# First norm's statistics from a second copy of the input, sums issued first, two convolutions held back, and the first output chunks by token halves

## The chip, the cores and the metric

The kernel runs on one core of a Trainium2 chip. Times are device microseconds of one launch. The kernel before took 2095.43 us as the median of three runs (2094.10 to 2096.46); a share of one thousandth is 2.1 us. The profiled execution is a run of its own.

The engines are named as the profile names them: PE is the matrix engine (PEld its weight loads), DVE the vector engine, ACT the scalar engine, POOL the general one, SP the one that issues the weight loads. Each works through its own list of instructions in order, and waits on the others by semaphores.

## The reference, cut to what matters

A decoder trunk of two layers on 256 tokens with 2048 features, in float32. Only the first mixer is touched by the change:

```python
u = rmsnorm(h, mix_pre_g[0])                       # h = x, 256 tokens by 2048
proj = u @ w_in                                    # 2048 by 3*2048
xin, gate_c, gate_b = jnp.split(proj, 3, axis=-1)
v = gate_c * xin
conv = sum(conv_w[k] * vp[:, k:k + S] for k in range(3))   # vp: v shifted right by 2, causal
m = (gate_b * conv) @ w_out
h = h + rmsnorm(m, mix_post_g[0])

def rmsnorm(x, g):
    return x * rsqrt(mean(x * x, axis=-1) + 1e-6) * g
```

Behind it come a squared-ReLU MLP (2048 to 8192 and back), the shared keys and values, stick-breaking attention and a second MLP. None of these is changed.

The factor `1/rms` of a token is the same for all features, so it commutes with the product by `w_in`. The kernel multiplies `x*g` by `w_in`, and scales afterwards: `gate_b` by r, and `gate_c*xin` by r squared, where r is the token's `1/rms`.

## The kernel before, in words

**Numbers in two parts.** Every float32 factor is split into a rounded high part and a remainder. ACT makes the high part of a weight chunk (`whi`, line 176), DVE the remainder (`wlo`, line 187). A chunk is 128 by 1024 numbers, 512 KB, loaded by SP into one of 5 `raw` buffers; 7 pairs of `whi`/`wlo` buffers hold split chunks and the splitting runs up to 4 chunks ahead of the product. So each chunk costs ACT and DVE one instruction over 128x1024 each.

**The input projection** (`convolution`) computes `w_in` with features on the partitions and the 256 tokens on the columns. Its units, in order:

- The **lead**: six column tiles of 128 features together, while the input arrives (k from 0 to 15, 12 chunks). Each lives in a bank of its own, banks 0 to 5.
- **Tiles 0 to 3**: one column tile each, two chunks each, in banks 0, 1, 7, 6.
- **Pair 0, tile 4, pair 1, tile 5, ... pair 15, tile 19.** A pair is two chunks of a second set of columns, computed with tokens on the partitions by a seven-product scheme. A pair needs four combinations of its weights (`sums`, line 213, DVE), their splits (`whi20a`, `b`, `t`, `u` for the pair whose first chunk is number 20), and four combinations of the input (`xs`, `xsums`). Eight pairs make a group, in banks 0 to 5 and 7; after pairs 7 and 15 DVE adds the group up (`mg<-mg,more` and `mg<-mg,acc`, line 988).
- **Tiles 20 to 25**, in banks 0, 1, 2, 0, 1, 3, with 16 transposes between tiles 21 and 22.

Tiles 3 to 19 share bank 6. A product with `whi` fills 512 columns (the input's high part and its remainder side by side), one with `wlo` 256, so a tile ends with `combined`: ACT copies the second half out (`half`, line 875), DVE adds it to the first (`sum`, line 877). The bank is free when that sum is done; the next tile in bank 6 starts one pair later. In tiles 0 and 2 and in tiles 20, 22 and 24 the `wlo` products stand ahead of the `whi` products.

**The convolutions.** Three sums (xin, gate_c, gate_b of one 128-feature block) go into `conv_tile`: a product (line 914), the scaling by r squared (921) and by r (926), the three taps (923 on ACT, 924, 925), the gate (927), and a split into the operand `y` (260 on ACT, 261). The eight blocks 0 to 7 come from the lead and tiles 0 to 17. The other eight come from tiles 18 to 25 (gates) and the pairs, after the transposes.

**Statistics.** While the lead runs, ACT squares the transposed input two feature blocks at a time (`sq`, line 891), DVE adds eight such tiles (`acc`, lines 893 and 895); then one addition (904), one product on PE with a matrix of 1/2048 (`ms`, 906), which sums over partitions and spreads the result, a root on ACT (908), a reciprocal (909) and a square (910) on DVE.

**The order.** On PE the order is the one in which the code is written. On DVE, ACT, POOL and SP a scheduler orders the instructions ahead of time, by the order of the code and by when its own model finds their inputs ready; `tc.high_priority()` lets an instruction pass others that are ready, `tc.issue_after(x)` puts it behind x.

**The output projection** (`project`, class `Mixed`) follows at once: chunks 96 to 127 of the stream, two groups of 16. For each chunk `both` calls `unit` for token half 0 (banks 0 and 1 in the first group) and then half 1 (banks 2 and 3); one half of a chunk is six products of 128x512.

Of the kernel before, what the change touches and what calls it, by code (L numbers as in the profile page):

```python
# [46 lines left out]
LATER = 7  # L47
# [3 lines left out]
DOWN_BANKS = {(0, 0): 3, (0, 1): 4, (1, 0): 5, (1, 1): UP_BANK, 1: 6, 5: 7, 6: 0, 7: 1}  # L51
LAST_BANKS = [[6, 7], [0, 1]]
OUT_MIXED = (((0, 1, 2, 5, 3, 6, 4, 7), (4, 6)), (tuple(range(KD // 2)), (3, 4)))
SEVEN = [((0, 1, 2, 3),) * 2] * (STEPS - 1) + [((0,), ())]
LOAD_FROM = 1
# [43 lines left out]
def trunk(ctx, tc, x, xT, vecs, rows, ws, out):  # L99
# [8 lines left out]
    wsplit = ctx.enter_context(tc.tile_pool(name="ws", bufs=RING))  # L108
    psum = ctx.enter_context(tc.tile_pool(name="ps", bufs=1, space=bass.MemoryType.PSUM))
# [250 lines left out]
    class Mixed(Group):  # L360


        def __init__(self, first, xs, banks, more, order, sevens_at, shared, evict):
            super().__init__(first, KD, xs, banks, self.add_and_evict)
            self.then, self.early = evict, 2 * sevens_at[-1] + 3 < KD - EDGE
# [12 lines left out]
        def both(self, i):  # L378
# [447 lines left out]
    def convolution(tmp):  # L826
# [27 lines left out]
        acc = tmp.tile([P, 2 * T], F32, tag="acc", name="acc", bufs=1)  # L854
# [17 lines left out]

        def combined(ps):
            b = tiny("half")
            nc.scalar.activation(b[:], ps[:, T:], AF.Copy)
            s = tiny("sum", bufs=LEAD + 2)
            nc.vector.tensor_tensor(s[:], ps[:, :T], b[:], op=ALU.add)  # L877
            return s
# [9 lines left out]
        def squares(q, behind):  # L888
            sq = tmp.tile([P, 2 * T], F32, tag="sq", name="sq", bufs=1)
            with tc.issue_after(entered[behind].ins):  # L890
                nc.scalar.activation(sq[:], hpair[q], AF.Square)
            if q == 0:
                nc.vector.tensor_copy(acc[:], sq[:])
            else:
                nc.vector.tensor_tensor(acc[:], acc[:], sq[:], op=ALU.add)

# [3 lines left out]
        mean = tmp.tile([P, P], F32, name="mean")  # L900
        nc.vector.memset(mean[:], 1.0 / D)

        def statistics():
            nc.vector.tensor_tensor(acc[:, :T], acc[:, :T], acc[:, T:], op=ALU.add)
            ps = bank(LEAD - 1, "ms")
            nc.tensor.matmul(ps[:, :T], mean[:], acc[:, :T], start=True, stop=True)
            r, r2 = tiny("rstd", bufs=1), tiny("rstd2", bufs=1)
# [25 lines left out]
        for k in range(KD):  # L933
# [12 lines left out]
            if k % 2 and LATER <= k + 2 < KD:  # L946
                squares((k + 2 - LATER) // 2, k + 2)
# [59 lines left out]
        for kind, i in IN_UNITS:  # L1007
# [23 lines left out]
            if i == KD + 3:  # L1031
                gated()
# [582 lines left out]
```

## Time and profile before

| what | value |
|---|---|
| runs, median (lowest to highest) | 2095.43 us (2094.10 to 2096.46) |
| profiled execution, its own time | 2094.54 us |
| its span, first to last instruction | 2092.7 us |
| granted PE clock | 0.999 |
| PE busy | 2079.6 us (99%) |
| DVE busy | 1896.7 us (91%) |
| ACT busy | 1466.4 us (70%) |
| end of the input projection, first product of the output projection | 269.48 us |

The busy times are shares of the whole span. The change touches the first 290 us or so, and there the question is which engine ends a wait last: an engine busy all the time can be the one that sets the pace, and PE can be the one that waits. In the answers of the trace, a row gives the start in us, the length, the engine, the line of the code, the instruction with output and inputs, and in brackets the idle time before it with the engine and line that ended it. Rows of one engine can overlap by about 0.08 us, since they are pipelined; the distance between two starts is what an instruction costs.

### The profile page before, as it was taken

The numbers are of one execution on the slowest core, as the hardware profiler recorded it, in microseconds if no ns is written. First come the engines' busy times: TensorE is split into PE (matmuls) and PEld (weight loads), VectorE is DVE, ScalarE is ACT, GpSimd is POOL, SyncE is SP. The second block draws the span as 40 slices with busy tenths as digits, with TensorE's granted clock in tenths as the row PEclk, the third lists the DMA queues.
The fourth block names the chain that finished last, engine by engine and source line by source line (L and its number), as shares of the span: only waits on it lengthen the run. The fifth ranks groups of instructions, "written<-read, shape, count | busy, mean of one in ns | idle before, by whom it ended". The sixth has DMA issues, their size and how long they took to land.

```text
span 2092.7 us, 29773 instructions
## 1 busy us (share of the span) xinstructions
PE 2079.6 (99%) x10564; PEld 1773.3 (85%) x10564; DVE 1896.7 (91%) x2822; ACT 1466.4 (70%) x2150; POOL 114.7 (5%) x141
## 2 busy tenths in 40 slices
PE   9999999999999999999999999999999999999998
PEld 7888888888888888888888888889888888888887
DVE  8999998999999999999766777558999999999996
ACT  8666556777777777777567888547877777777774
POOL 0000000000100101101000000000001010010010
PEclk9999999999999999999999999999999999999999
DMA  8466675677878878779575555665687787787884
GB/s 293 150 205 210 200 268 178 194 232 227 241 218 237 236 216 252 227 230 259 180 223 163 161 161 162 220 181 171 187 254 228 221 247 222 230 245 218 232 241 165
DMA packets 132917, 449.23 MB, mean 215 GB/s; under 512 B 14880, under 2 KB 15136, under 8 KB 132256
## 3 DMA queue, kind: packets, MB, share of 16 engines
q1 hardware_dynamic: 113328, 406.68, 60.8%
q0 software_dynamic: 19296, 40.38, 9.7%
q8 instruction: 83, 1.36, 0.3%
q14 instruction: 66, 0.54, 0.1%
q10 hardware_dynamic: 144, 0.26, 0.0%
HBM read 413.19 MB, written 2.10 MB: 198 GB/s over the span
## 4 chain that ended last, share of the span: by engine, by line
PE 96%; DVE 3%; issue 1%; DMA 0%; ACT 0%; SPq 0%; DVEq 0%; ACTq 0%
PE up L1138 21%; PE up L1145 12%; PE acc L334 7%; PE acc L336 7%; PE acc L335 7%; PE acc L868 5%; PE more L1252 5%; PE more L1251 5%; PE more L1253 5%; PE acc L1251 4%; PE acc L1252 4%; PE acc L1253 4%; PE lead L868 1%; PE up L1140 1%; PE tr L266 1%; DVE wlo L187 1%
## 5 line engine op out<-in xcount | busy, mean ns | idle before, releaser
L187 DVE TENSOR_TENSOR wlo<-raw,whi 128x1024 fp32r<-128x1024 f32 (+1 forms) x410 | 489.2, 1201 | 54.0 <-ACT whi L176 53.3
L176 ACT ACTIVATE whi<-raw 128x1024 fp32r<-128x1024 f32 (+1 forms) x410 | 421.4, 1044 | 139.9 <-PE acc L336 46.6
L1138 PE MATMUL up<-u,whi 128*128 128x512 f32 x1952 | 465.0, 389 | 0.0
L1138 PEld LDWEIGHTS up<-u,whi 128*128 128x128 f32 x1952 | 365.0, 188 | 74.7
L1145 PEld LDWEIGHTS up<-u,wlo 128*128 128x128 f32 x2048 | 263.6, 191 | 10.3
L1145 PE MATMUL up<-u,wlo 128*128 128x256 f32 x2048 | 268.0, 283 | 0.0
L213 DVE TENSOR_TENSOR sums<-raw,sums 128x512 f32<-128x512 f32 x260 | 177.3, 682 | 0.9
L189 DVE SCALAR_TENSOR_TENSOR wlo<-raw,gv,whi 128x512 fp32r<-128x512 f32 (+1 forms) x160 | 131.8, 853 | 41.5 <-ACT whi L176 40.8
L176 ACT ACTIVATE whi<-raw,gv 128x512 fp32r<-128x512 f32 (+1 forms) x160 | 121.6, 800 | 48.4 <-PE acc L336 42.0
L334 PE MATMUL acc<-whi,u 128*128 128x512 f32 x384 | 153.1, 399 | 0.1
L336 PE MATMUL acc<-whi,u 128*128 128x512 f32 x384 | 149.9, 390 | 0.0
L335 PE MATMUL acc<-wlo,u 128*128 128x512 f32 x384 | 149.7, 390 | 0.0
L1151 ACT ACTIVATE half<-up 128x256 f32<-128x256 f32 x128 | 49.1, 385 | 132.9 <-PE up L1145 130.4
L1158 POOL DMA_DIRECT2D mg<-more x108 | 94.0, 870 | 824.4 <-ACT more L1213 422.4
L868 PE MATMUL acc<-u,whi 128*128 128x512 f32 x416 | 98.9, 391 | 2.8 <-DVE sum L877 2.8
L868 PEld LDWEIGHTS acc<-u,whi 128*128 128x128 f32 x416 | 77.4, 188 | 20.5 <-DVE sum L877 3.7
L213 DVE TENSOR_TENSOR sums<-raw,raw 128x512 f32<-128x512 f32 x130 | 88.7, 682 | 3.8 <-DMA raw<-w_mlp 3.5
L213 DVE TENSOR_TENSOR sums<-raw 128x512 f32<-128x512 f32 x130 | 88.6, 681 | 1.3 <-DMA raw<-w_mlp 1.1
L336 PEld LDWEIGHTS acc<-whi,u 128*128 128x128 f32 x384 | 72.1, 188 | 15.5
L334 PEld LDWEIGHTS acc<-whi,u 128*128 128x128 f32 x384 | 72.2, 188 | 13.9 <-ACT tk L1446 0.6
L335 PEld LDWEIGHTS acc<-wlo,u 128*128 128x128 f32 x384 | 72.3, 188 | 13.3
L868 PEld LDWEIGHTS acc<-u,wlo 128*128 128x128 f32 x416 | 52.8, 191 | 3.8 <-DVE sum L877 2.1
(6789 smaller groups left out, 4607.0 us busy)
## 6 DMA issues: line engine op xcount, KB each, us to landing
raw<-w_mlp SPq DMA_DIRECT2D x512, 512.0 KB, 4.7
raw<-w_in SPq DMA_DIRECT2D x94, 512.0 KB, 4.4
mg<-more POOLq DMA_DIRECT2D x108, 256.0 KB, 6.1
raw<-w_out SPq DMA_DIRECT2D x32, 512.0 KB, 4.6
raw<-w_v SPq DMA_DIRECT2D x32, 512.0 KB, 4.3
raw<-w_k SPq DMA_DIRECT2D x32, 512.0 KB, 4.2
raw<-w_q SPq DMA_DIRECT2D x32, 512.0 KB, 3.8
raw<-w_wo SPq DMA_DIRECT2D x32, 512.0 KB, 3.7
```

The lines of the kernel that those rows point to most:

```text
L176: rounded = nc.scalar.activation(hi[:, at], raw[i][:, at], AF.Copy, scale=1.0 if gain is None else gain)
L187: nc.vector.tensor_tensor(lo[:, at], t[:, at], hi[:, at].bitcast(F32), op=ALU.subtract)
L213: nc.vector.tensor_tensor(t, x, y, op=ALU.subtract)
L334: nc.tensor.matmul(ps[:], xh, hi[:, a], start=first, stop=False, skip_group_check=skip)
L335: nc.tensor.matmul(ps[:], xh, lo[:, a], start=False, stop=False, skip_group_check=skip)
L336: self.done = nc.tensor.matmul(ps[:], xl, hi[:, a], start=False, stop=last, skip_group_check=skip)
L868: nc.tensor.matmul(ps[:, :cols], w, xs[:, :cols], start=k == 0 and part == parts[0], stop=k == KD - 1 and part == parts[1], skip_group_che ...
L1138: nc.tensor.matmul(ps, weight(0, first, m), x, start=k == 0, stop=False)
L1145: nc.tensor.matmul(pss[n][:, :T], weight(1, first, m), x, start=False, stop=k == KD - 1)
L1251: nc.tensor.matmul(self.ps[key][:], xh, hi, start=first, stop=False)
L1252: nc.tensor.matmul(self.ps[key][:], xh, lo, start=False, stop=False)
L1253: self.done = nc.tensor.matmul(self.ps[key][:], xl, hi, start=False, stop=last)
```

## The change

- **Statistics.** The squares of the transposed input, their additions, the product on PE, and the reciprocal over 128x256 are gone. The input is loaded a second time, as rows (tokens on the partitions), in four pieces of 512 KB from POOL's queue, each held behind the `half` of tile 0, 1, 1 and 2. ACT squares a piece in place and adds up along it (two pieces behind the `half` of tile 2, two behind that of tile 3). Two columns of sums are added, rooted and inverted per 128 tokens (128x1 each), turned by 32x32 transposes, written as a line of 256 numbers to a scratch tensor in DRAM, and read back to all partitions. Behind the `half` of tile 5 ACT makes r and r squared of it.
- **Sums.** In `combined`, both instructions get high priority.
- **Convolutions.** Three sums are put in a list; from tile 5 on, a convolution is taken from it per tile while more than two wait, from tile 20 on while any waits. Before, blocks 0, 2, 1, 3, 4, 5, 6, 7 were done at tiles 1, 2, 4, 5, 8, 11, 14, 17. Now blocks 0 to 7 are done at tiles 5, 6, 8, 11, 14, 17, 20, 21. The ring of sums has 12 buffers in place of 8.
- **Output projection.** In its first group, the first two chunks are done for token half 0 and then for half 1, in place of chunk by chunk.

```diff
-LATER = 7
+ROWS_AT = {0: (0,), 1: (1, 2), 2: (3,)}
+SQUARES_AT = {2: (0, 1), 3: (2, 3)}
+STATISTICS_AT = 3
+HELD = 2
+TURN = 32
...
+            self.first_by_half = not shared["sums"] and banks[0][0] == 0
...
-            if p not in self.at:
+            if p not in self.at and (i > 1 or not self.first_by_half):
                 super().both(i)
+            elif i == 0:
+                self.unit(0, 0)
+            elif i == 1:
+                self.unit(0, 1)
+                for n in range(2):
+                    self.unit(1, n)
...
         def combined(ps):
             b = tiny("half")
-            nc.scalar.activation(b[:], ps[:, T:], AF.Copy)
-            s = tiny("sum", bufs=LEAD + 2)
-            nc.vector.tensor_tensor(s[:], ps[:, :T], b[:], op=ALU.add)
+            with tc.high_priority():
+                copied["last"] = nc.scalar.activation(b[:], ps[:, T:], AF.Copy)
+            s = tiny("sum", bufs=LEAD + 6)
+            with tc.high_priority():
+                nc.vector.tensor_tensor(s[:], ps[:, :T], b[:], op=ALU.add)
             return s
...
+        def load_piece(q, behind):
+            b, c = q // 2, q % 2
+            if c == 0:
+                xrows.append(act.tile([P, D], F32, tag="x4", name="xrows"))
+            load = nc.gpsimd.dma_start(
+                xrows[b][:, c * D // 2 : (c + 1) * D // 2], x[b * P : (b + 1) * P, c * D // 2 : (c + 1) * D // 2]
+            )
...
+        def square_piece(q, behind):
...
+            a = xrows[b][:, c * D // 2 : (c + 1) * D // 2]
+            with tc.issue_after(behind.ins):
+                nc.scalar.activation(a, a, AF.Square, accum_out=sq[b][:, c : c + 1])
+
         def statistics():
-            nc.vector.tensor_tensor(acc[:, :T], acc[:, :T], acc[:, T:], op=ALU.add)
-            ps = bank(LEAD - 1, "ms")
-            nc.tensor.matmul(ps[:, :T], mean[:], acc[:, :T], start=True, stop=True)
-            r, r2 = tiny("rstd", bufs=1), tiny("rstd2", bufs=1)
-            nc.scalar.activation(r[:], ps[:, :T], AF.Sqrt, bias=eps[:])
-            nc.vector.reciprocal(r[:], r[:])
-            nc.vector.tensor_tensor(r2[:], r[:], r[:], op=ALU.mult)
-            scale["r"], scale["r2"] = r, r2
+            line = scratch.tile([1, T], F32, name="line")
+            turn = tmp.tile([P, NB * TURN], F32, name="turn")
+            with tc.high_priority():
+                for b in range(NB):
+                    nc.vector.tensor_tensor(sq[b][:, 0:1], sq[b][:, 0:1], sq[b][:, 1:2], op=ALU.add)
+                    r = inverse_root(sq[b][:, 0:1], eps[:])
+                    nc.vector.tensor_copy(roots[:, b * TURN : b * TURN + 1], r[:])
+                nc.vector.transpose(turn[:], roots[:])
+            nc.gpsimd.dma_start(
+                line[:].rearrange("o (b a t) -> (o a) b t", b=NB, t=TURN), turn[0:P:TURN, :].rearrange("a (b t) -> a b t", b=NB)
+            )
+            scale["all"] = tiny("rstd", bufs=1)
+            nc.gpsimd.dma_start(scale["all"][:], line[:].to_broadcast([P, T]))
+
+        def scales(behind):
+            r = scale["all"]
+            scale["r"], scale["r2"] = tiny("rstd1", bufs=1), tiny("rstd2", bufs=1)
+            with tc.issue_after(behind.ins):
+                nc.scalar.activation(scale["r"][:], r[:], AF.Copy)
+                nc.scalar.activation(scale["r2"][:], r[:], AF.Square)
...
-            if not scale:
+            s = combined(ps)
+            for q in ROWS_AT.get(i, ()):
+                load_piece(q, copied["last"])
+            for q in SQUARES_AT.get(i, ()):
+                square_piece(q, copied["last"])
+            if i == STATISTICS_AT:
                 statistics()
-            s = combined(ps)
+            if i == STATISTICS_AT + 2:
+                scales(copied["last"])
...
-                if lead and len(new) == 2:
-                    conv_tile(LEAD // 3 - len(lead) // 3, *lead[:3])
-                    del lead[:3]
                 if len(new) == 3:
-                    conv_tile(n - 2 * KD, *new)
+                    waiting.append((n - 2 * KD, *new))
                     new = []
+            if i >= STATISTICS_AT + 2 and len(waiting) > (0 if i >= KD + 4 else HELD):
+                conv_tile(*waiting.pop(0))
```

What this does to the lists, at two places. **DVE at the end of the lead** (`lead` names the lead's banks, the number behind `wlo` is the chunk). Before:

```order
L895 TENSOR_TENSOR acc_113<-acc_113,sq_479 128x512
L187 TENSOR_TENSOR wlo15_541<-raw15_407,whi15_540 128x1024
L895 TENSOR_TENSOR acc_113<-acc_113,sq_482 128x512
L187 TENSOR_TENSOR wlo16_547<-raw16_431,whi16_546 128x1024
L904 TENSOR_TENSOR acc_113<-acc_113 128x256
L187 TENSOR_TENSOR wlo17_561<-raw17_454,whi17_560 128x1024
L877 TENSOR_TENSOR sum_487<-lead_125,half_485 128x256
L877 TENSOR_TENSOR sum_491<-lead_126,half_489 128x256
```

Now:

```order
L279 TENSOR_TENSOR xs_648<-xa_645 128x128
L279 TENSOR_TENSOR xs_648<-xs_648,xa_645 128x128
L192 TENSOR_TENSOR wlo15_518<-raw15_396,whi15_517 128x1024
L279 TENSOR_TENSOR xs_648<-xa_645,xs_648 128x128
L192 TENSOR_TENSOR wlo16_524<-raw16_420,whi16_523 128x1024
L892 TENSOR_TENSOR sum_464<-lead_126,half_462 128x256
L892 TENSOR_TENSOR sum_468<-lead_127,half_466 128x256
L892 TENSOR_TENSOR sum_472<-lead_128,half_470 128x256
L953 TENSOR_TENSOR sum_464<-sum_464,sum_468 128x256
L192 TENSOR_TENSOR wlo17_538<-raw17_440,whi17_537 128x1024
```

The additions of squares are gone, the split of chunk 17 stands behind the first three sums, and two more sets of input combinations (`xs`, `xsums`) stand ahead of them than before.

**DVE from the sum of tile 20 on** (chunks 90 and 91 are tile 23, 92 and 93 tile 24; the first `sum` row of each piece is that of tile 20). Before:

```order
L877 TENSOR_TENSOR sum_2516<-acc_2469,half_2514 128x256
L187 TENSOR_TENSOR wlo90_2520<-raw90_2421,whi90_2519 128x1024
L187 TENSOR_TENSOR wlo91_2534<-raw91_2435,whi91_2533 128x1024
L919 MEMSET v_2589 128x2
L926 TENSOR_TENSOR sum_2369<-sum_2369,rstd_593 128x256
L919 MEMSET v_2602 128x2
L926 TENSOR_TENSOR sum_2463<-sum_2463,rstd_593 128x256
L926 TENSOR_TENSOR sum_2516<-sum_2516,rstd_593 128x256
L187 TENSOR_TENSOR wlo92_2640<-raw92_2474,whi92_2639 128x1024
L187 TENSOR_TENSOR wlo93_2654<-raw93_2488,whi93_2653 128x1024
L877 TENSOR_TENSOR sum_2565<-acc_2518,half_2563 128x256
```

Now, the first rows and, some 40 rows further on, those around chunks 92 and 93:

```order
L892 TENSOR_TENSOR sum_2493<-acc_2446,half_2491 128x256
L953 TENSOR_TENSOR sum_1751<-sum_1751,sum_1846 128x256
L958 MEMSET v_2496 128x2
L965 TENSOR_TENSOR sum_1941<-sum_1941,rstd1_1016 128x256
L960 TENSOR_TENSOR v_2496<-sum_1751,rstd2_1017 128x256
L192 TENSOR_TENSOR wlo90_2509<-raw90_2398,whi90_2508 128x1024
L963 SCALAR_TENSOR_TENSOR conv_2499<-v_2496,gv_83,conv_2499 128x256
L192 TENSOR_TENSOR wlo91_2523<-raw91_2412,whi91_2522 128x1024
```

```order
L266 TENSOR_TENSOR y4_2600<-sum_2440,y4_2600 128x256
L266 TENSOR_TENSOR y4_2600<-sum_2493,y4_2600 128x256
L960 TENSOR_TENSOR v_2627<-tr_2573,rstd2_1017 128x128
L965 TENSOR_TENSOR sum_2554<-sum_2554,rstd1_1016 128x256
L192 TENSOR_TENSOR wlo92_2641<-raw92_2451,whi92_2640 128x1024
L963 SCALAR_TENSOR_TENSOR conv_2631<-v_2627,gv_83,conv_2631 128x256
L192 TENSOR_TENSOR wlo93_2655<-raw93_2465,whi93_2654 128x1024
L892 TENSOR_TENSOR sum_2748<-acc_2701,half_2746 128x256
```

Before, the splits of tile 24 stood ahead of the sum of tile 21. Now the held convolutions of blocks 6 and 7 and three convolutions of transposed blocks stand ahead of them, and the sums of tiles 21 and 22 too.

More of the change, by code (lines that the diff above doesn't have):

```diff
@@ L901, in convolution @@
[L901 to L911 removed]
+        xrows, sq = [], []
@@ new lines, in convolution @@
+        roots = tmp.tile([P, NB * TURN], F32, name="roots")
+        nc.vector.memset(roots[:], 0.0)
+        def load_piece(q, behind):
[5 more added lines that the diff above has]
+            )
+            tc.add_manual_dep(
+                load.ins, behind.ins.name,
+                mybir.DependencyInfo(mybir.DependencyClass.Sync, mybir.DependencyReason.DATA), reason="later",
+            )
@@ L945, in convolution @@
             mm([(ps, k, n) for ps, n in zip(pss, IN_N[:LEAD])], lambda k, n: at_lead[k, n])
[L946 to L949 removed]
         lead = [combined(ps) for ps in pss]
+        waiting = [(i, *lead[3 * i : 3 * i + 3]) for i in range(LEAD // 3)]
         stores = [stream_x.tile([P, 4, 2, NB, P], F32R, tag="h", name="xsums") for _ in range(NB)]
```

20 lines of the change are left out of this document (7 added, 13 removed).

## The prediction, made before the changed kernel ran

> **What bounds the kernel now.** First the page's busy shares, then the busy time by stages of the input projection, then what PE waited for over the whole span, then PE's rows at those waits.
>
> ```profile
> PE 2079.6 (99%) x10564; PEld 1773.3 (85%) x10564; DVE 1896.7 (91%) x2822; ACT 1466.4 (70%) x2150; POOL 114.7 (5%) x141
> ```
>
> ```profile
> 42.17:70.63 28.46, 27.75 (x151) 23.96 (x152) 28.07 (x64) 19.63 (x36) 0.00 (x0) 1.00 0.45 139
> 70.63:103.36 32.73, 31.55 (x159) 26.40 (x159) 32.73 (x52) 19.64 (x26) 0.00 (x0) 1.00 0.53 173
> 144.81:176.00 31.19, 30.33 (x155) 25.43 (x154) 31.19 (x45) 17.46 (x23) 0.00 (x0) 1.00 0.55 175
> 228.86:269.48 40.62, 40.62 (x242) 36.18 (x240) 39.38 (x85) 22.89 (x35) 0.00 (x0) 1.00 0.57 188
> ```
>
> The columns are the stage, its length, the busy time of PE, PEld, DVE, ACT and POOL, PE's granted clock, DMA share and GB/s. PE is the bound of the whole: only 13 us of the 2092.7 are idle. But in the first three of these stages DVE is busy to the last tenth and PE is not; there DVE sets the pace. After 176 us PE never waits until the tail.
>
> ```profile
> PE acc L868 <- DVE sum L877: 4.7, 5, 1.9
> PE end L776 <- ACT roots L775: 1.4, 1, 1.4
> ```
>
> So what a change of this stage can win is the five waits of a column tile for the sum that frees its bank, and little else. At them PE's rows are:
>
> ```profile
> 39.37 0.87 PE L868 MATMUL lead<-u,wlo 128*128 128x256 f32 x6
> 42.17 2.18 PE L868 MATMUL acc<-u,wlo 128*128 128x256 f32 x16 [1.94 <-DVE sum L877]
> 47.85 0.59 PE L906 MATMUL ms<-acc,mean 128*128 128x256 f32 x2
> 48.09 0.58 PE L868 MATMUL acc<-u,whi 128*128 128x512 f32 x1
> 69.53 0.39 PE L979 MATMUL acc<-whi20u,u 128*128 128x512 f32 x1
> 70.63 3.87 PE L868 MATMUL acc<-u,whi 128*128 128x512 f32 x16 [0.71 <-DVE sum L877]
> 91.14 0.39 PE L979 MATMUL acc<-whi28u,u 128*128 128x512 f32 x1
> 91.86 0.50 PE L868 MATMUL acc<-u,whi 128*128 128x512 f32 x1 [0.33 <-DVE sum L877]
> 102.12 0.39 PE L979 MATMUL acc<-whi32u,u 128*128 128x512 f32 x1
> 103.36 3.93 PE L868 MATMUL acc<-u,whi 128*128 128x512 f32 x16 [0.85 <-DVE sum L877]
> 165.51 0.39 PE L979 MATMUL acc<-whi56u,u 128*128 128x512 f32 x1
> 166.76 0.50 PE L868 MATMUL acc<-u,whi 128*128 128x512 f32 x1 [0.86 <-DVE sum L877]
> ```
>
> Products of 512 columns start 0.23 us apart, so the true gaps are from the last start plus 0.23: 70.63 - 69.76 = 0.87, then 0.49, 1.01 and 1.02, together **3.39**. The first gap is 42.17 - (39.37 + 0.87) = **1.93**. The `ms` product costs 48.09 - 47.85 = **0.24**.
>
> **Term 1, the sum at the end of the lead.** These are DVE's groups from 10.94 to the first sum at 41.70, and the last rows ahead of it:
>
> ```profile
> L187 DVE TENSOR_TENSOR wlo<-raw,whi 128x1024 fp32r<-128x1024 f32 x16 | 19.3, 1219 | 0.3 <-ACT whi L176 0.3
> L895 DVE TENSOR_TENSOR acc<-acc,sq 128x512 f32<-128x512 f32 x7 | 4.8, 684 | 0.0
> L274 DVE TENSOR_TENSOR xs<-xa 128x128 f32<-128x128 f32 x4 | 1.1, 286 | 0.1
> ```
>
> ```profile
> 40.23 0.42 DVE L904 TENSOR_TENSOR acc<-acc 128x256 f32<-128x256 f32 x1
> 40.57 1.22 DVE L187 TENSOR_TENSOR wlo<-raw,whi 128x1024 fp32r<-128x1024 f32 x1
> 41.70 0.42 DVE L877 TENSOR_TENSOR sum<-lead,half 128x256 f32<-128x256 f32 x1
> 39.91 0.91 ACT L875 ACTIVATE half<-lead 128x256 f32<-128x256 f32 x3
> ```
>
> From start to start an instruction costs 0.08 less than its mean: 1.14, 0.60, 0.34 and 0.20 for 1024, 512, 256 and 128 columns. DVE had no gap there, so the sum was late by its queue. Out go seven additions, one copy and one last addition (4.2 + 0.34 + 0.34 = 4.9) and one split that now stands behind (1.14); in come two sets of input combinations, nine of 0.20 and two of 0.60 by the count of rows (3.0). The queue is 3.0 shorter and free at 38.7; then the sum waits for its inputs instead. The first bank's last product ends near 39.5, ACT's copy takes 0.3, the sum 0.34: the bank is free at about 40.2, when PE ends the lead. I leave 0.3 of the 1.93 for the handover (bounds 0 and 0.9) and take **-1.6**. ACT loses eight squares of 0.5 in this stretch and is not late.
>
> **Term 2, the four sums of tiles 3, 5, 6 and 12.** Bank 6 is needed again one pair (21 x 0.23 = 4.8 us) after a tile ends, so a sum may be 4.8 late, not more. Tile 3:
>
> ```profile
> 64.97 0.40 PE L977 MATMUL more<-whi20a,u 128*128 128x512 f32 x1
> 70.07 0.41 DVE L877 TENSOR_TENSOR sum<-acc,half 128x256 f32<-128x256 f32 x1
> ```
>
> The sum started 5.1 after the tile's end at 64.97. From the first lead sum (41.70) to it DVE worked 28.4 without a gap. Counted over the list of the change, the same stretch holds 21.9: two convolutions fewer, 5.0, whose price is in these rows (0.34, 0.34, 0.33 for the three products, 0.40 for a tap, 0.34 for gate and split);
>
> ```profile
> 63.31 0.41 DVE L914 TENSOR_TENSOR sum<-sum 128x256 f32<-128x256 f32 x1
> 63.65 0.41 DVE L926 TENSOR_TENSOR sum<-sum,rstd 128x256 f32<-128x256 f32 x1
> 63.98 0.41 DVE L921 TENSOR_TENSOR v<-sum,rstd 128x256 f32<-128x256 f32 x1
> 48.98 1.75 DVE L909 RECIPROCAL rstd<-rstd 128x256 f32<-128x256 f32 x1 [0.39 <-ACT rstd L908]
> ```
>
> the reciprocal with its wait and the square, 2.4; three sets of combinations already done, 4.2; against it one split, four weight combinations and a product that moved in, 3.9 (the other small rows, some 1 us, even out). So DVE reaches tile 3's sum at 40.2 + 21.9 = 62.1, and the tile ends at 40.3 + 4 x 5.55 = 62.5: not late at all. From there the list holds 8.9, 10.1, 10.0, 11.2 and 9.4 us of DVE work to the sums of tiles 4 to 8, 49.6 against five PE periods of 10.33 = 51.6, and at worst a sum is 1.5 late. At tile 12 seven group additions come in (4.2); they now stand around chunk 52's splits, and I count that sum 1.5 late too. So all four gaps go: **-3.4**. With no relief at all the term would be 0.
>
> **Term 3.** The `ms` product goes: **-0.2**.
>
> **What is added and hidden.** The row loads come from POOL; the nearest rows are the same 512 KB issued there later, and the 256 KB additions, with their issue time and landing; the last row prices ACT over 1024 columns:
>
> ```profile
> h<-x POOLq DMA_DIRECT2D x4, 512.0 KB, 5.8
> L1158 POOL DMA_DIRECT2D mg<-more x108: 860/869/895, 451.3 to 2042.2; - x108
> DMA to landing us min/median/max: 3.3/6.2/8.5
> L176 ACT ACTIVATE whi<-raw 128x1024 fp32r<-128x1024 f32 (+1 forms) x410 | 421.4, 1044 | 139.9 <-PE acc L336 46.6
> ```
>
> Pieces 1 and 2 leave at tile 1's copy (52.2) and land near 59, piece 3 near 64; ACT's squares at 58 and 63 wait 0 to 3 us, cost 4 x 1.0, and delay the splits for tile 4, which PE needs at 67.3. ACT is 60 to 70% busy there and nothing ahead of 67.3 hangs on it; without that cover the 4 us would count. The line goes out near 70 and is back after two transfers, 2 x (0.9 + 6.2) = 14 at most like the rows above, at 84; ACT asks for it at 84. DVE's and ACT's small 128x1 rows are under 1 us in all, inside the counts above. The by-half order of chunks 96 and 97 issues the same 24 products; it needs chunk 97's split 1.4 earlier and banks 2 and 3 1.4 later: 0.
>
> **Term 4, what the held convolutions do at the end.** Blocks 6 and 7 now fall on tiles 20 and 21, where DVE still had cover:
>
> ```profile
> 240.59 0.42 DVE L877 TENSOR_TENSOR sum<-acc,half 128x256 f32<-128x256 f32 x1 [0.47 <-ACT half L875]
> 244.22 2.35 DVE L187 TENSOR_TENSOR wlo<-raw,whi 128x1024 fp32r<-128x1024 f32 x2
> 236.32 7.44 PE L868 MATMUL acc<-u,whi 128*128 128x512 f32 x32
> 256.45 4.00 PE L868 MATMUL acc<-u,wlo 128*128 128x256 f32 x32
> ```
>
> Tile 24's splits were ready at 246.5 and used from 258.3 (half of the last row), 12 us early. Tile 20 ends at 236.32 + 3.65 = 239.97, tile 24 starts 18.3 later. In the new list 18.0 us of DVE work stand between tile 20's sum (done 0.95 after the tile) and the end of chunk 93's split, and I count 0.8 of waiting for ACT: ready at 19.8, used at 19.3. Since tile 24 begins with its `wlo` products, PE waits: **+0.5**. Chunks 96 to 103 follow with 1.4 to 3 us of margin where there were 7: **+0.2**. Bounds 0 and 5 (both convolutions in full).
>
> **Sum.** -1.6 - 3.4 - 0.2 + 0.7 = -4.5 against the profiled 2094.5: 2090.0. The median of the runs stands 0.9 above that execution, so the forecast for a median is **2090.9**. With the bounds: at best -1.9 - 3.4 - 0.2 = -5.5, at worst -1.0 - 3.4 - 0.2 + 5 = +0.4, so 2089.9 to 2095.8 for that case.
>
> **Rivals.** *The wait moves to the splits* (0.2): term 4 at 2 to 5 us. For it: DVE's list from tile 20 to chunk 104 is longer than PE's time by about what it had spare, and ACT's queue stands between each step. Against: the count gives 0.7. Price: 2092.3 to 2095.4, around 2093. *The change does not free DVE* (0.1): the splits wait for raw buffers and these for DVE, so that sums issued first are answered by late splits and only terms 1 and 3 come, 2093.6. Against: in the 52.86 us behind 176 us, with the same work per period, PE has no wait.
>
> *Slower by the late factors* (0.1): ACT's copy of r stands in order; if the line comes back at 84 + x, splits behind it and DVE's first convolution stop too. PE has some 5 us of split chunks ahead; from x = 5 each further us is PE's, from x = 9.5 (a round trip of 23.5 us) the change loses, and at x = 14, twice the rows, it ends at 2090.9 + 9 = 2099.9. For it: POOL's transfers landed in up to 8.5 us. The Trainium skill, "DMA: Bandwidth & Descriptors", section "Anatomy of one DMA", speaks against this step too: the receipt of a write takes most of a fixed 2.0 us per transfer, longest where DRAM is the target; its fit of 2.0 us plus bytes over 436 GB/s gives an estimate of 4.3 us for both transfers, where the rows give 14; no run so far shows a transfer of this size, and by either figure the line is there by 84.
>
> **Chances.** Forecast 0.6, rivals 0.2, 0.1, 0.1. Two thousandths, 4.2 us, is about what a measurement here can tell; that is 2091.2. The forecast lies just beyond it, so of its 0.6 some 0.47 is faster, the rest and the first two rivals same: faster 0.47, same 0.43, slower 0.10. The range 2088.6 to 2095.8 leaves out the slower case and a tail below, where DVE's relief also closes small gaps that I did not count.
>
> **What would show it.** PE's wait for `sum` falls from 4.7 to below 1; `ms` is gone; tile 4 starts near 67; a new wait of under 1 us for `wlo` at tile 24, near 253; the output projection starts near 265. Wrong if `sum` still stops PE between 60 and 170, if ACT idles for `xrows` or the line while PE waits, or if the start at 265 is lost again before 300.

## The result, and the profile after

| kernel | median | lowest to highest | runs |
|---|---|---|---|
| before | 2095.26 us | 2094.10 to 2097.15 | 20 |
| changed | 2091.01 us | 2089.90 to 2095.37 | 20 |

The changed kernel takes 0.998 of the time before (95% interval 0.9974 to 0.9986): 4.25 us less. Its profiled execution took 2090.84 us, with a span of 2089.1. The first view is the page of busy shares, then what PE waited for over the span:

```profile
PE 2078.8 (100%) x10562; PEld 1774.0 (85%) x10562; DVE 1891.6 (91%) x2818; ACT 1467.5 (70%) x2153; POOL 117.4 (6%) x147
```

```profile
PE end L788 <- ACT roots L787: 1.4, 1, 1.4
PE acc L339 <- DVE acc L453: 0.9, 1, 0.9
PE acc L879 <- DVE sum L892: 0.3, 1, 0.3
PE acc L879 <- DVE wlo L192: 0.3, 1, 0.3
```

The 4.7 us of waiting for `sum` are 0.3. Two waits are new: one for a split (`wlo`) and one for an addition (`acc`, line 453). PE's rows at the old places and the new ones:

```profile
39.85 0.87 PE L879 MATMUL lead<-u,wlo 128*128 128x256 f32 x6
41.06 2.18 PE L879 MATMUL acc<-u,wlo 128*128 128x256 f32 x16 [0.34 <-DVE sum L892]
...
67.95 0.39 PE L1015 MATMUL acc<-whi20u,u 128*128 128x512 f32 x1
68.17 3.79 PE L879 MATMUL acc<-u,whi 128*128 128x512 f32 x16
...
250.67 3.40 PE L879 MATMUL acc<-u,wlo 128*128 128x256 f32 x24
254.32 1.22 PE L879 MATMUL acc<-u,wlo 128*128 128x256 f32 x8 [0.26 <-DVE wlo L192]
255.37 7.44 PE L879 MATMUL acc<-u,whi 128*128 128x512 f32 x32
...
264.56 0.39 PE L339 MATMUL acc<-whi,y 128*128 128x512 f32 x1
...
337.97 0.39 PE L341 MATMUL acc<-whi,y 128*128 128x512 f32 x1
339.23 0.47 PE L339 MATMUL acc<-whi,y 128*128 128x512 f32 x1 [0.87 <-DVE acc L453]
```

Tile 4 (68.17) follows its pair without a gap. The last row is in the second group of the output projection: its bank was wanted at 338.2 and an addition (`add_total`) still stood in DVE's queue. In DVE's rows of both kernels, first before, then after:

```profile
340.94 1.22 DVE L187 TENSOR_TENSOR wlo<-raw,whi 128x1024 fp32r<-128x1024 f32 x1
342.07 1.88 DVE L441 TENSOR_TENSOR acc<-acc,more 128x512 f32<-128x512 f32 x3
```

```profile
337.26 1.22 DVE L192 TENSOR_TENSOR wlo<-raw,whi 128x1024 fp32r<-128x1024 f32 x1
338.39 1.89 DVE L453 TENSOR_TENSOR acc<-acc,more 128x512 f32<-128x512 f32 x3
```

PE's same product stood 4.92 us earlier than before (264.56 against 269.48 at the start of the projection), the addition only 3.68 earlier (338.39 against 342.07).

**Where PE lost time, by stretch.** The lead ends at 40.24 before and 40.72 after. I take that difference for chance and not for a part of the change: the lead's products are alike, and over the 14 profiles of this study its end lies between 40.19 and 41.25. So everything below is counted from the lead's end. I took the first row of PE at six places and subtracted the shortest length that any of the 14 profiles has for that stretch (22.32, 176.34, 23.96 and 63.26 us from tile 0 on):

| lost, us | before tile 0 | tile 0 to chunk 20 | chunk 20 to transposes | to output projection | to chunk 120 | at the addition | sum |
|---|---|---|---|---|---|---|---|
| before | 1.93 | 0.48 | 4.20 | 0.01 | 0.01 | 0 | 6.6 |
| changed | 0.34 | 0 | 0.01 | 0.87 | 0.18 | 0.87 | 2.3 |

The change wins 6.3 us up to the transposes and gives 1.9 back behind them: 4.4 net, close to the measured 4.25. The two profiled executions are 3.70 us apart (2094.54 and 2090.84): of the 4.36 the later end of the lead takes 0.48, and 0.2 are lost behind 340 us, at places that I did not follow.

### The profile page after: what moved, and what is told of

It is laid out like the page before. It is cut to its first block, busy times and chain, and to the rows that moved or that the text cites. A ratio compares the mean times of both kernels' runs of the same rounds, so it can differ in the third digit from the quotient of the medians.

```text
span 2089.1 us, 29770 instructions
## 1 busy us (share of the span) xinstructions
PE 2078.8 (100%) x10562; PEld 1774.0 (85%) x10562; DVE 1891.6 (91%) x2818; ACT 1467.5 (70%) x2153; POOL 117.4 (6%) x147
## 4 chain that ended last, share of the span: by engine, by line
PE 98%; DVE 1%; DMA 1%; ACT 0%; SPq 0%; issue 0%; ACTq 0%
PE up L1179 21%; PE up L1186 12%; PE acc L339 7%; PE acc L341 7%; PE acc L340 7%; PE acc L879 6%; PE more L1293 5%; PE more L1292 5%; PE more L1294 5%; PE acc L1292 4%; PE acc L1293 4%; PE acc L1294 4%; PE lead L879 1%; PE up L1181 1%; PE tr L271 1%; PE more L1014 1%
```

## The experiments

Each row of the next table is the profiled execution of one experiment, counted in the same way; the ratio is to the kernel before, measured beside it. The experiments ran in three rounds, on three chips; the kernel before had medians of 2096.20 (the first: none held, sums not first, sums first alone, one held), 2095.28 (the second: old statistics, chunk order, staged, late line) and 2095.16 us (the third: the rest). So a median of one round is compared with one of another through the ratios.

| experiment | before tile 0 | to chunk 20 | to transposes | to projection | to chunk 120 | at the addition | sum | median | ratio (95%) |
|---|---|---|---|---|---|---|---|---|---|
| old statistics | 1.95 | 2.04 | 0 | 2.13 | 0.01 | 0.88 | 7.0 | 2094.39 | 0.9995 (0.9986 to 1.0004) |
| none held | 0.34 | 0.01 | 6.48 | 0.01 | 0.13 | 0 | 7.0 | 2093.49 | 0.9990 (0.9981 to 0.9998) |
| sums not first | 0.34 | 0 | 0 | 1.27 | 1.94 | 0 | 3.6 | 2091.74 | 0.9983 (0.9974 to 0.9992) |
| chunk order | 0.34 | 0 | 0 | 1.76 | 0.01 | 0.76 | 2.9 | 2091.70 | 0.9980 (0.9971 to 0.9989) |
| sums first alone | 1.81 | 0.48 | 3.74 | 0 | 3.90 | 0 | 9.9 | 2097.06 | 1.0006 (0.9997 to 1.0015) |
| one held | 0.34 | 0 | 1.51 | 0.58 | 0 | 0 | 2.4 | 2091.11 | 0.9977 (0.9968 to 0.9986) |
| staged | 0.34 | 0.01 | 0.24 | 1.71 | 0 | 0.17 | 2.5 | 2091.66 | 0.9985 (0.9976 to 0.9994) |
| load early | 0.34 | 0 | 1.34 | 5.79 | 0 | 0 | 7.5 | 2094.67 | 0.9996 (0.9987 to 1.0005) |
| load late | 0.34 | 0 | 0.01 | 5.48 | 0.01 | 0.28 | 6.1 | 2094.17 | 0.9994 (0.9986 to 1.0003) |
| product on POOL | 0.35 | 0 | 0.04 | 0 | 4.47 | 0 | 4.9 | 2093.41 | 0.9989 (0.9980 to 0.9998) |
| before, product on POOL | 1.97 | 2.00 | 5.48 | 0.01 | 0 | 0 | 9.5 | 2097.39 | 1.0010 (1.0001 to 1.0018) |
| late line | 0.34 | 0 | 8.18 | 1.49 | 0.01 | 0.76 | 10.8 | 2099.28 (one run) | |

One profile is one execution: where PE stalled for about 2 us its clock sometimes halved behind the stall (last section), and then the profile can show more than a typical run.

### One part undone

**Old statistics** goes back, in the changed kernel, to the squares of the transposed input in the lead, the `ms` product, and the root and reciprocal over 128x256; the second copy, the pieces' squares and the line are gone.

```diff
-            if i == STATISTICS_AT:
-                statistics()
+            if not scale:
+                statistics()
```

> The changed kernel with the old statistics (squares of the transposed input in the lead, the product on PE, the reciprocal over 256 columns), the held convolutions, the sums first and the by-half order kept. Theory (both parts free DVE, and it is the splits around chunk 52 that run dry next): the wait at the end of the lead is back (1.6 us more than with the change), the product 0.24; DVE's list holds 3.0 us more from tile 3 on, about what one convolution is, so 1.5 to 2 us are lost at chunks 52 to 60 as with one convolution held; the wait at 339 us goes. About 2093.5. Rival, the holding is enough: only the 1.8 us, 2092.0 to 2092.9. Rival, the statistics are what frees DVE: 3 us or more are lost between tiles 3 and 19, 2095.

The wait at the end of the lead is back, and nothing is lost from chunk 20 to the transposes, not the 1.5 to 2 us that I expected there. So the four waits of term 2 stay away without the new statistics. Nor did the wait at the addition go, as I expected: it is 0.88. The 2.04 lost ahead of chunk 20 are the old product on PE and, for most of it, the clock, which fell to half for 3.4 us behind the stall at the lead. What the old statistics add on DVE comes out behind the transposes, at tile 24, where two waits stand in place of one:

```profile
42.72 3.12 PE L880 MATMUL acc<-u,wlo 128*128 128x256 f32 x16 [1.95 <-DVE sum L893]
257.21 1.18 PE L880 MATMUL acc<-u,wlo 128*128 128x256 f32 x8 [0.78 <-DVE wlo L193]
259.25 1.22 PE L880 MATMUL acc<-u,wlo 128*128 128x256 f32 x8 [0.86 <-DVE wlo L193]
```

**None held.**

```diff
-HELD = 2
+HELD = 0
```

> The changed kernel with no convolution held back: from tile 5 on one is done per tile while any waits, so blocks 0 to 7 fall on tiles 5, 6, 7, 8, 9, 11, 14, 17 and none on tiles 20 and 21. Theory: the two convolutions at tiles 20 and 21 are what stops PE for 0.26 us at tile 24 and for 0.87 us at 339 us; without them both waits go, sums come at most 3.6 us behind their tiles by the list (4.8 allowed), and 2089.9. Rival: holding back is what freed DVE; with 5 us more work ahead of tile 10, waits for sums or splits of 1 us or more come back between 90 and 180 us, 2092 or more.

The rival held: with the new statistics but nothing held back, PE runs dry at chunk 52, right behind the seven group additions on DVE:

```profile
148.00 0.50 PE L1014 MATMUL more<-wlo52a,u 128*128 128x512 f32 x1 [1.97 <-DVE wlo52a L192]
149.74 0.80 PE L1014 MATMUL acc<-wlo52b,u 128*128 128x512 f32 x1 [0.71 <-DVE wlo52b L192]
```

Both late waits are gone, and the stretch loses 6.48 us in this profile (by the ratios a typical run takes some 2 us more than the change). That is more than the 2.68 of the two waits; most of the rest is the clock (last section).

**Sums not first.**

```diff
-            with tc.high_priority():
-                copied["last"] = nc.scalar.activation(b[:], ps[:, T:], AF.Copy)
+            copied["last"] = nc.scalar.activation(b[:], ps[:, T:], AF.Copy)
...
-            with tc.high_priority():
-                nc.vector.tensor_tensor(s[:], ps[:, :T], b[:], op=ALU.add)
+            nc.vector.tensor_tensor(s[:], ps[:, :T], b[:], op=ALU.add)
```

> The changed kernel without the high priority of copy and sum. Load theory: the relief of DVE by the statistics and the held convolutions takes the four waits away by itself; the two lists are alike up to tile 10, so PE waits under 0.5 us for sums, and 2091.0 within 0.3. Order theory: the waits of 0.5 to 1.0 us at tiles in bank 6 come back, 2 us or more together, 2093 or more.

The load theory held: no wait for a sum up to the transposes. Behind them the priority matters. Tile 25's sum comes late and stops the second token half:

```profile
270.35 0.47 PE L339 MATMUL acc<-whi,y 128*128 128x512 f32 x1 [1.50 <-DVE sum L890]
```

In exchange the wait at the addition is gone. By the ratios the priority is worth 0.6 us, less than these runs can tell.

**Chunk order.**

```diff
-            self.first_by_half = not shared["sums"] and banks[0][0] == 0
+            self.first_by_half = False
```

> The changed kernel without the by-half order of the first two chunks of the output projection. DVE and ACT keep their lists. As the prediction costs it: 0, so 2091.0 and no new wait. By the trace after: the sum that frees bank 3 starts at 266.40 and ends near 266.8, while the chunk order asks for that bank 2.06 us behind the start of the output projection (the priority experiment showed its wait there), at 266.62, in place of 3.43 us behind it: PE waits 0.4 at 266.6. DVE gains that time, so the wait at 339 us shrinks by as much, from 0.9 to 0.5, and the time stays at 2091.0. If the wait at 339 us comes from the by-half order, it vanishes whole.

No wait for the bank came near 266.6. The sum that frees it started at 266.01, as far behind the lead as with the change (225.8 against 225.7), but this profile lost 0.9 more at tile 24, and PE came that much later. The prediction's 0 for this edit stands within the interval. At the addition 0.76 of the wait are left, so the by-half order is not what causes it.

### One part alone

**Sums first alone**, on the kernel before:

```diff
-            nc.scalar.activation(b[:], ps[:, T:], AF.Copy)
-            s = tiny("sum", bufs=LEAD + 2)
-            nc.vector.tensor_tensor(s[:], ps[:, :T], b[:], op=ALU.add)
+            with tc.high_priority():
+                nc.scalar.activation(b[:], ps[:, T:], AF.Copy)
+            s = tiny("sum", bufs=LEAD + 2)
+            with tc.high_priority():
+                nc.vector.tensor_tensor(s[:], ps[:, :T], b[:], op=ALU.add)
```

> The kernel before with one edit: the copy and the sum of a column tile get high priority. Old statistics, old convolutions. Load and order theory (the prediction's): with the old load on DVE the list still brings the sums of tiles 7 to 14 to 4.8 to 6.6 us behind their tiles, where 4.8 is allowed, so 0 to 1.8 of the 3.4 us of term 2 stay as waits, the 1.9 us at the end of the lead and the 0.24 us product stay too: PE waits 1.9 to 3.7 us for sums, 2092.2 to 2093.7. Order alone theory: issuing sums first is enough, PE waits for sums only at the end of the lead, 1.9, and 2091.9. Load alone theory: DVE is as overloaded as before, so 4.7 us of waits stay, for sums or for splits, 2095.3.

This is nearest to load alone. PE's waits for sums of tiles in bank 6 are gone from the list:

```profile
PE acc L334 <- DVE sum L879: 2.0, 1, 2.0
PE acc L868 <- DVE sum L879: 1.8, 1, 1.8
PE acc L980 <- DVE wlo32b L187: 0.2, 1, 0.2
PE acc L980 <- DVE wlo56b L187: 0.2, 1, 0.2
```

Yet the stretch from chunk 20 to the transposes loses 3.74 us, against 4.20 before. The four visible stalls have become many short ones, for splits, most of them too short for the list. Then tile 25's sum stops PE for 2.0 at the start of the projection. A wait that leaves the list of waits need not have left the time.

### Where the held convolutions go

**One held** and **staged** let them go earlier, one at a time:

```diff
-HELD = 2
+HELD = 1
```

```diff
-len(waiting) > (0 if i >= KD + 4 else HELD)
+len(waiting) > (0 if i >= KD + 4 else 1 if i >= KD + 2 else HELD)
```

> The changed kernel with one convolution held back in place of two (blocks on tiles 5, 6, 7, 8, 11, 14, 17, 20). Theory: 2.5 us less of DVE work behind tile 20; the addition that PE waits for at 339 us came 1.24 us later behind PE's place than before with 0.37 us of margin, so half of the work is enough to lose it: no wait at 339 us, none at tile 24, 2089.9. Rival (the by-half order or something else causes the wait at 339 us): it stays at 0.9, 2091.0.

> The changed kernel with the held convolutions let go one by one: two are held up to tile 17, one from tile 18, none from tile 20 (blocks 6 and 7 on tiles 18 and 20 in place of 20 and 21). Theory: the tight place at chunks 52 to 60 keeps both convolutions out, and 2.5 us of DVE work are back in the stretch from tile 18 to 20; the output projection starts as with the change (223.8 us behind the lead), the wait for the split at tile 24 goes; the wait at 339 us falls only by what DVE idles less, 0 to 0.9. 2090.0 to 2090.9. Rival: DVE has no room between tiles 18 and 20 either, splits stop PE there by 1 us or more, 2092.

Both expected a gain near 1 us and neither shows one. With one held the wait at the addition is gone and 1.5 us are lost near chunks 52 to 60; staged, it is 0.17 and tile 24 costs 1.7. The start of the addition on DVE, counted from the lead's end, hardly moves: 297.67 with the change, 297.70 and 297.86 here, though PE started the projection 1.2 and 1.1 us later. With the chunk order and with sums not first it is 298.3 and 298.8. So as long as PE is not stopped for long on the way, it is DVE that sets when the addition comes. (With none held, where PE stopped near chunk 52 and its clock halved, the addition starts at 302.2 with the same work on DVE.) Its stretch from the lead's end to the addition, before, with the change and with old statistics:

```profile
40.24:342.07 301.83, 297.14 (x1507) 252.92 (x1508) 294.25 (x466) 184.85 (x253) 4.40 (x8) 1.00 0.65 210
```

```profile
40.72:338.39 297.67, 296.90 (x1509) 253.56 (x1508) 289.80 (x458) 187.53 (x256) 7.70 (x14) 1.00 0.67 219
```

```profile
40.77:343.18 302.41, 298.77 (x1510) 255.35 (x1510) 294.55 (x466) 186.73 (x253) 4.40 (x8) 0.99 0.65 210
```

The third busy time is DVE's. It works 289.8 of 297.7 us; before, 294.3 of 301.8. The change takes 4.5 us of work from it and the addition comes 4.2 earlier.

The work is not all of it. Of the 1.5 us that DVE idles between the start of the projection and the addition, 1.32 are one wait, and it ends with a transfer:

```profile
304.50 1.06 ACT L181 ACTIVATE whi<-raw 128x1024 fp32r<-128x1024 f32 x1 [1.57 <-DMA raw<-w_out]
305.59 1.23 DVE L192 TENSOR_TENSOR wlo<-raw,whi 128x1024 fp32r<-128x1024 f32 x1 [1.32 <-ACT whi L181]
```

SP issued that weight chunk at 299.16, as soon as DVE had freed a `raw` buffer, and it landed at 304.42. The wait is longer than PE's 0.87 at 339, so an earlier chunk might have taken that away with the same work on DVE. No run tests this.

### Load added to DVE

That gave a new theory: over the whole stretch DVE has next to no reserve (it idles 7.9 of 297.7 us), so that its work counts wherever it stands. **Load early** and **load late** add seven additions to the changed kernel, whose result nobody uses, behind tile 8 (as shown) or tile 18:

```diff
+            if i == 8:
+                for _ in range(7):
+                    nc.vector.tensor_tensor(pad[:], pad[:], s[:], op=ALU.add)
```

> The changed kernel with 2.4 us more work on DVE (seven additions over 128x256, 0.34 us each, into a spare tile) behind the sum of tile 8. New theory: from the end of the lead to the addition at 339 us DVE is the bound as a whole (by the profiles it was busy 290 of 298 us there, and the start of that addition behind the lead, 297.7, stayed when PE's waits ahead of it moved), so any work added to it ends up in the time, wherever it stands: that addition starts 2.4 us later, 2093.4. Rival (only the stalls that PE shows count, as the prediction reckoned them): the stretch between chunks 52 and 60 loses 1.5 us as with one convolution held, and wins the wait of 0.9 at 339 us back, 2091 to 2092.

> The same 2.4 us of DVE work behind the sum of tile 18. New theory: the same 2.4 us in the time, 2093.4, the addition at 339 us starts 2.4 us later behind the lead. Rival (only the stalls that PE shows count): no wait stands between tiles 18 and 23, so it is hidden there, and tile 24's wait grows by at most 1 us: 2091 to 2092.

The work is in the time at both places: 2094.67 and 2094.17, by the ratios some 3 us above the change and not the rival's 2091 to 2092. That this is more than the 2.4 us added is within the interval. But the addition did not start 2.4 us later, as expected. It started 302.97 and 301.53 behind the lead, 5.3 and 3.9 later: DVE's busy time rose by 2.2 and 2.5 (to 292.0 and 292.3), and its idle time grew too, from 7.9 to 10.9 and 9.3. Behind PE's stall and its halved clock the tiles ended later, and DVE waited for them (3.03 us at 265.4 with the load early). In the profiles the work surfaces at tile 24, first early, then late:

```profile
255.49 1.24 PE L879 MATMUL acc<-u,wlo 128*128 128x256 f32 x8 [1.94 <-DVE wlo L192]
257.26 2.08 PE L879 MATMUL acc<-u,wlo 128*128 128x256 f32 x8 [0.53 <-DVE wlo L192]
```

```profile
255.92 1.22 PE L879 MATMUL acc<-u,wlo 128*128 128x256 f32 x8 [3.37 <-DVE wlo L192]
257.36 2.08 PE L879 MATMUL acc<-u,wlo 128*128 128x256 f32 x8 [0.22 <-DVE wlo L192]
```

The second row of each takes 2.08 where the same eight products take 1.22 in the changed kernel: the halved clock again.

### Load taken from DVE

**Product on POOL** and **before, product on POOL** move one multiplication of each of the 16 convolutions:

```diff
-            nc.vector.tensor_tensor(sb[:], sb[:], scale["r"][:], op=ALU.mult)
+            nc.gpsimd.tensor_tensor(sb[:], sb[:], scale["r"][:], op=ALU.mult)
```

> The changed kernel with the scaling of gate_b by r (128x256, 16 of them, 0.34 us each on DVE) on POOL, which only issues transfers there. New theory: DVE has 5.4 us less, the addition at 339 us comes early enough, its wait of 0.9 and most of that at tile 24 go, and then PE is the bound: 2089.9. If POOL's products slow DVE's down or come late for the product that follows, less: 2091 or more.

> The kernel before with that scaling on POOL, nothing else. New theory: DVE has 5.4 us less up to the addition at 342 us, so PE's four waits between 70 and 167 us (3.4) and nothing else go; the 1.9 at the end of the lead and the 0.24 us product stay: 2091.9. Rival (only the sums' lateness at their tiles counts): the list brings the sums of tiles 5 to 12 only 1.0 to 2.1 us earlier, so 1.3 of the 3.4 us stay, 2093.2. If the order is what matters: 2095.

Both came out slower than the new theory had them: with the change, the branch held by which POOL slows DVE down (2091 or more), and in the kernel before none did. They do not test the theory, since DVE was not relieved. While POOL multiplies, some of DVE's instructions take up to about twice as long. The first row is POOL's, the others DVE's, of the changed kernel with the product on POOL:

```profile
85.22 4.00 POOL L965 TENSOR_TENSOR sum<-sum,rstd 128x256 f32<-128x256 f32 x4 [10.57 <-ACT rstd L949]
```

```profile
86.25 1.22 DVE L218 TENSOR_TENSOR sums<-raw,sums 128x512 f32<-128x512 f32 x1
87.40 1.22 DVE L192 TENSOR_TENSOR wlo32a<-raw,whi32a 128x512 fp32r<-128x512 f32 x1
89.42 0.68 DVE L218 TENSOR_TENSOR sums<-raw,sums 128x512 f32<-128x512 f32 x1
```

DVE's busy time up to the addition rose from 289.8 to 290.9 us although 16 multiplications had left it, and in the kernel before from 294.3 to 295.7.

### The late factors

**Late line** puts six more transfers between the written line and its spread:

```diff
+            for n in range(6):
+                line, last = scratch.tile([1, T], F32, name=f"line{n}"), line
+                nc.gpsimd.dma_start(line[:], last[:])
```

> The changed kernel with six more copies of the line of 256 factors in DRAM, one behind the other, ahead of its spread to all partitions. By the trace after (1 KB landed 2.1 us behind its issue, 2.4 us per copy) the factors come back near 93 us in place of 79; in this kernel ACT asks for them near 91 us, since the scheduler saw the delay and moved the request by some 6 us. The prediction's rival (PE is hurt from the time the factors are 5 us later than asked, each further us is PE's): at 2 to 3 us late nothing is lost, 2091.0. If DVE and ACT have no cover at all, PE loses these 2 to 3 us, 2093 to 2094.

The copies were slower than I reckoned: the factors were there at 99.1, 9.3 us behind ACT's request and not 2 to 3.

```profile
99.10 0.42 ACT L953 ACTIVATE rstd<-rstd 128x256 f32<-128x256 f32 x1 [9.34 <-DMA rstd<-line]
```

```profile
103.95 6.80 PE L880 MATMUL acc<-u,whi 128*128 128x512 f32 x16 [5.00 <-DVE sum L893]
```

Behind the waiting instruction on ACT stood the copy (`half`) of tile 6, and PE wanted that tile's bank. PE stalled 5.0 us, and the tile behind it took 6.80 in place of 3.9. With x = 9.3 the prediction's rival would have cost x - 5 = 4.3; the stall is near that, but with the clock the stretch lost 8.2.

## Why the prediction was right, and where it was not

The forecast was 2090.9 and the median is 2091.01. By its own steps, counted from the lead's end:

- **Term 1**, -1.6: the gap went from 1.93 to 0.34, -1.59. DVE was free before the sum's input was there, as predicted (it idles 0.60 for ACT's copy), and the old statistics alone bring 1.95 back. This term belongs to the statistics.

```profile
40.58 1.09 DVE L892 TENSOR_TENSOR sum<-lead,half 128x256 f32<-128x256 f32 x3 [0.60 <-ACT half L889]
```

- **Term 2**, -3.4: the four gaps are gone, and with smaller ones that I had not counted the stretch won 4.2. But I gave the relief to the whole list at once. The runs say which part it is: with the two convolutions held and the old statistics (sums first kept) nothing is lost there; with the new statistics and nothing held, 6.5. The statement that tile 3's sum would be "not late at all" was wrong: it started 1.7 us behind the tile's end (63.38 and 65.08). The count added up DVE's work and left out its waits for inputs, 1.07 at 51.58 and 0.93 at 57.33; the allowed 4.8 hid that. (The 28.4 us "without a gap" of the kernel before held one too, the 0.39 in the prediction's own row at 48.98.)
- **Term 3**, -0.2: the stretch around the product won 0.48.
- **Term 4**, +0.7: 0.87 at tile 24, at the place named and for the reason named, and 0.18 up to chunk 120. The trace lists only 0.26 of it as a wait; most of the rest hides in a row of grouped products (250.67).
- **What failed** is the sentence of term 4 that ended the count at "chunks 96 to 103". The held work does not end there. From 224.0 us behind the lead's end, where the changed kernel starts the projection, to the addition DVE idled 1.5 us, against 5.9 before, and 0.87 came out at 339. With it the term is 1.9 and not 0.7. The bounds of 0 to 5 held it, the sum did not name it.
- **Hidden work**: the line left at 71.94 and its spread at 74.31, landing 4.6 later, so the factors were there at 78.9 and ACT asked at 84.5. The round trip was 7.0 us where I took 14 as a bound. The Trainium skill, "DMA: Bandwidth & Descriptors", section "Anatomy of one DMA", gave 4.3 as an estimate for both. Its 2.0 us fits the written line (2.1 from issue to landing); for the spread its fit gives 2.3 as an estimate, and the trace has 4.6. The by-half order was put at 0, and the chunk order in its place took the same time within the interval.
- **Rivals.** The wait did move to the splits and to the addition, by 1.9 us and not by 2 to 5; that is nearer to this rival's 2 than to the 0.7 of the forecast. That DVE is not freed is refuted for the whole (4.5 us less work), and so is the slow case here: the factors came 5.6 us early. By the late line its price was too low, because it left out the clock.

Summed up: -1.59 - 0.48 - 4.19 + 0.86 + 0.17 + 0.87 = -4.36, against -4.5 predicted and -4.25 measured; terms 2 and 3 gave 1.1 more than I took, and term 4 took 1.2 back. That the sum came so close is luck; the signs, the places of the first waits and the sizes of terms 1 and 2 are not. That the addition's lateness comes from DVE's total work, and not from the two held convolutions as such, is supported by four runs (one held, staged, both loads). It is not proven from the side of relief: the runs that were to take work from DVE did not do so. And the wait for a weight chunk at 305 stands beside it untested.

No version here beats the changed kernel beyond what the runs can tell; one held (2091.11) is its equal.

## What to carry to other kernels

Work that is held back on a nearly full engine is borrowed time: count the list on to the next place where somebody waits for that engine, not only to where the work is done. When a reordering removes a wait, compare the length of the stretch and not the list of waits, because one stall can come back as many that are too short to be listed. A sum of an engine's work is a lower bound for when it is done: its waits for inputs come on top. Before moving work to an idle engine, look at how long the busy one's instructions take while the other runs.

## What the runs showed of the hardware

**A stall of some 2 us can halve PE's clock, and where it falls decides.** These are four stretches of 3.41 us around chunk 52 with none held. The first number behind the length is PE's busy time, and the one ahead of the last two is the granted clock:

```profile
145.35:148.76 3.41, 1.44 (x8) 0.84 (x6) 3.41 (x7) 1.56 (x3) 0.00 (x0) 1.00 0.02 6
148.76:152.18 3.42, 2.71 (x7) 1.98 (x7) 3.42 (x4) 3.42 (x5) 0.00 (x0) 0.50 0.61 188
152.18:155.59 3.41, 3.41 (x10) 2.67 (x9) 3.41 (x7) 1.19 (x2) 0.00 (x0) 0.50 0.72 268
155.59:159.00 3.41, 3.41 (x17) 2.78 (x16) 3.41 (x8) 1.64 (x3) 0.00 (x0) 1.00 0.48 161
```

While the clock was at half the products stood 0.43 us apart and not 0.23, which cost about as much as the stall. Ahead of the tail it followed stalls of 1.94 (with load early), 1.95, 1.97 (twice), 1.98, 2.55, 3.37 and 5.00 us, and not those of 1.94 in the kernel before and of 2.37 in the one with its product on POOL, nor any of 1.81 or less.

The clock's records in the traces say why. Between two changes the clock always stays for a whole multiple of 3.41 us (at half 3.41 five times and 6.83 three times; at full, for instance, 37.55, which is 11 steps, 143.36, which is 42, or 266.24, which is 78). So it changes only on a grid of that step, which lies elsewhere in every execution. Cut into these windows, all 14 profiles follow one rule, the tail included: a window at full clock in which PE idles 1.94 us or more is followed by half clock, and one with 1.80 or less is not. The stall of 1.94 in the kernel before was cut by a border of the grid into 1.80 and 0.14:

```profile
38.62:42.03 3.41, 1.62 (x10) 1.25 (x9) 3.41 (x5) 3.14 (x6) 0.00 (x0) 1.00 0.91 327
42.03:45.45 3.42, 3.28 (x22) 3.06 (x23) 3.42 (x9) 2.48 (x6) 0.00 (x0) 1.00 0.87 305
```

The 2.37 was cut into 1.56 and 0.81. The 1.94 of load early lay in one window whole. Ahead of the tail the clock came back behind a half window with at most 0.22 us of idling, and stayed at half for a second one behind 0.53, 0.60 and 0.71. By this rule the stall at the end of the lead must in some executions of the kernel before cost about 1.5 us more than in the profile shown, as it did in the profiles of old statistics and of before with its product on POOL (2.04 and 2.00 lost up to chunk 20, against 0.48); how many, no run here shows.

The Trainium skill, "TensorE: Matmul & The Clock Gate", section "Part 1: The HAM clock gate (the "warmup" mystery)", has the clock fall to half after an idle window of about 3.4 us, on windows that run freely. The half rate, the length of the window and its running freely agree with these records; that the whole window must be idle does not, since 1.94 us of it were enough here.

**POOL's arithmetic slows DVE.** The Trainium skill, "SBUF — State Buffer", section "SBUF: two separate sides", says that a DVE instruction with two inputs from that memory and a POOL one lock the same ports against each other. The rows agree in direction: 1.22 for 0.68 us while POOL ran four products in 4.0 us. Not every instruction beside POOL was slowed; some of the same shape kept their 0.68.
